# Routed experts on one core: tokens gathered for two units at once from a rounded and a rest part, biases by single-pass matmuls, eight places for weights

## The chip, the core and the metric

The kernel runs on one core of a Trainium2 chip. The metric is the device time of one execution in microseconds (us). The engines are TensorE (PE in the rows, its weight loads PEld), VectorE (DVE), ScalarE (ACT), GpSimd (POOL) and SyncE (SP), whose queue issues nearly all DMAs.

## The reference

One inference step of one layer on 384 tokens of width 1024 (128 context tokens, 256 latent tokens). The part that matters here is the expert sub-layer:

```python
logits = xt @ router_w + router_b
top_val, top_idx = lax.top_k(logits, 4)          # of 32 experts
gates = softmax(top_val)
# for each expert e, the tokens that chose it:
h = xblk @ w_gu[e] + b_gu[e]                      # 1024 -> 2048
x_glu, x_lin = split(h, 2)                        # both clipped at 7
act = x_glu * sigmoid(1.702 * x_glu) * (x_lin + 1)
y = act @ w_down[e] + b_down[e]                   # 1024 -> 1024
# y times the gate, summed per token; then x = LN(ALPHA * x + gate2 * y)
```

Ahead of it stand the conditioning, the mLSTM and Fourier heads and a first LayerNorm. Everything is f32; the weights of the 32 experts are 32 x 12.6 MB, read once.

## The kernel before

**Two phases.** The first some 240 us hold everything up to the router. The rest runs the experts in order of their load (`ORDER`), each with a fixed number of places for tokens: 128, 96, 64 or 32. Experts are packed into 17 units of 128 rows. Unit 0 holds two experts of 64; the others follow the string DACBACBACBACACCE: A is one expert of 128, B 96 + 32, C 64 + 64, D 64 + 32 + 32, E four of 32.

**A unit.** `marks` (DVE) writes a one-hot matrix `O`, token by place. `gather` multiplies it with the normalised tokens `tX`: for each of 8 groups of 128 channels, 3 token blocks, in plain f32; `modulate` (ACT for the first half, DVE for the second) applies scale and shift into `XT`. Unit 0 is gathered at the end of phase 1 (L985, XT0). A closure that `gather` returns, here called the spreader, transposes `O` and picks the gate values.

**An expert.** `gate_up` runs 8 channel steps (L1119), then adds the bias by matmuls (L1126) that pick the expert's row of `bgu` with a column of `PmQ`, broadcast. An expert has one or two "parts": parts of 64 rows use half of PE's columns and 512-column matmuls (n=2), parts of 32 rows a quarter and 256-column ones (n=4). Then `act`, the transposes (L1151), `down` (L1177) and the evictions (L1183 on ACT, L1185 on DVE). When a unit is complete `spread` (L1194, single pass) adds it into `yacc`.

**Weights.** They stream through nine places of 2 MB: pools ringh (two halves), ringq (2), ringr (1) and ringp (5), in a rotating list `rings`; four pieces per expert of w_gate_up, two of w_down. `load_gu` and `load_dn` issue them on SP in program order (L755), and each waits there for the last matmul that reads the place. The first expert's w_down has its second half in two other tiles (L781, L782).

**Order.** The program's order sets each engine's order. Matmuls are f32 (several passes inside) unless both operands are fp32r tiles, which take one pass; a value split into a rounded part and the rest then takes two matmuls.

Of the kernel before, what the change touches and what calls it, by code (L numbers as in the profile page):

```python
# [20 lines left out]
D = 1024  # L21
# [75 lines left out]
def tile_layer(ctx, tc, x_prompt, x_sample, state_C, state_n, state_m, c, c_ctx, w_ada, b_ada, w_in,  # L97
# [47 lines left out]
    tX = keep.tile([128, NB, D], FT, name="tX")  # L145
# [22 lines left out]
    SP.dma_start(tX[:, 1:3], x_sample.rearrange("o (b p) d -> p (o b) d", p=128))  # L168
# [21 lines left out]
    for i, w in enumerate(ada0):  # L190
        for a in range(2):
            SP.dma_start(w[:, :, 256 * a:256 * a + 256],
                         w_ada[0, :, 1024 * a + 256 * i:1024 * a + 256 * i + 256].rearrange("(k p) n -> p k n", p=128))
        if i == 0:
            SP.dma_start(tX[:, 0], x_prompt[0])
# [61 lines left out]
    with tc.tile_pool(name="psA", bufs=1, space=PSUM, reuse_waits="tile") as psA:  # L257
# [7 lines left out]
        def pos_x(b, hf):  # L265
# [3 lines left out]
            a = tX[:, b, hf * 512:hf * 512 + 512]  # L269
# [15 lines left out]
        def x_T(b):  # L285
            for q in range(2):
                p = bankA().rearrange("p (j n) -> p j n", j=4)
                for j in range(4):
                    PE.transpose(p[:, j], tX[:, b, (4 * q + j) * 128:(4 * q + j + 1) * 128], ident)
# [436 lines left out]
    PmQ = late.tile([128, 4, NE], FT, name="PmQ")  # L726
# [62 lines left out]
    def modulate(XT, i, pl, pc):  # L789

        for jj in range(4):
            j = 4 * i + jj
            if i:
                DVE.tensor_scalar(XT[:, j], pl[:, jj], aff[:, 1, j:j + 1], aff[:, 0, j:j + 1], op0=OP.mult, op1=OP.add)
            else:
                ACT.activation(XT[:, j], pl[:, jj], AF.Identity, bias=aff[:, 0, j:j + 1], scale=aff[:, 1, j:j + 1])
        DVE.tensor_add(XT[:, 4 * i:4 * i + 4], XT[:, 4 * i:4 * i + 4], pc)
# [27 lines left out]
    Pm = PmQ[:, 0]  # L825
    POOL.memset(PmQ, 0.0)
# [3 lines left out]
    with tc.tile_pool(name="psC", bufs=2, space=PSUM, reuse_waits="tile") as psC:  # L830
# [27 lines left out]
        def out_half(b, i):  # L858
            p, x = Pj.pop((b, i)), tX[:, b, halves[i]]
# [13 lines left out]
        def out_norm(b):  # L873
# [35 lines left out]
        def turn(b, i):  # L909
            pu = pu0.pop() if pu0 else psC.tile([128, 4, 128], FT, name="pu")  # L910
            for j in range(4):
                PE.transpose(pu[:, j], tX[:, b, (4 * i + j) * 128:(4 * i + j + 1) * 128], ident)
# [41 lines left out]
        def sort_1():  # L954
# [4 lines left out]
            DVE.tensor_scalar(Pm[:32], cst[:32, C_ROP:C_ROP + NE], cl[:, 2:3], None, op0=OP.is_equal)  # L959
# [6 lines left out]
        def sort_1b():  # L966
# [5 lines left out]
            for q in range(1, 4):  # L972
                DVE.tensor_copy(PmQ[32 * q:32 * q + 32, q], Pm[:32])
# [6 lines left out]
        def gather_0(b, *js):  # L980
            for jj in range(*js):
# [3 lines left out]
                PE.matmul(t[:, jj % 4], tX[:, b, jj * 128:(jj + 1) * 128], O0[:, b], start=(b < 2 and jj % 4 == 0), stop=(b != 1),  # L985
# [58 lines left out]
        XT0 = mo.tile([128, 8, 128], FT, name="XT")  # L1044
        for i in range(2):
            modulate(XT0, i, xt[i], xc[i])
# [10 lines left out]
    def marks(sizes, ccol):  # L1057
        O = mo.tile([128, NB, 128], FT, name="O", bufs=1)[:, :, :sum(sizes)]
        i = at = 0
        while i < len(sizes):  # L1060
            n = sizes[i]
            e = next((q for q in range(len(sizes) - i) if sizes[i + q] != n), len(sizes) - i)
            DVE.tensor_tensor(O[:, :, at:at + e * n].rearrange("p b (e s) -> p b e s", e=e), iota(n, e),
                              ccol[:, :, i:i + e].unsqueeze(3).to_broadcast([128, NB, e, n]), op=OP.is_equal)
            i, at = i + e, at + e * n
        return O

    def gather(u, sizes, ccol, gcol_, XT=None, O=None):

        e, m = len(sizes), sum(sizes)  # L1070
        O = marks(sizes, ccol) if O is None else O
        if XT is None:
            XT = mo.tile([128, 8, 128], FT, name="XT")
            for i in range(2):
                pl, pc = (bank().rearrange("p (c n) -> p c n", c=4)[:, :, :m] for _ in range(2))
                for jj in range(4):
# [3 lines left out]
        OT = mo.tile([128, T], FR, name="OT", bufs=3)[:m]  # L1080
        gc = mo.tile([128, 4], FT, name="gc", bufs=3)
        parts, at, c_ = [], 0, 0
        for n in sizes:

            parts.append([(at + o, t, c_ + q, o) for q, (o, t) in enumerate(PARTS[n])])
            at, c_ = at + n, c_ + len(PARTS[n])
        U[u] = dict(XT=XT, OT=OT, gc=gc, m=m, parts=parts)

        def spreader():
            p = bank()  # L1090
# [5 lines left out]
            for i in range(e):  # L1096
                for o, n, c_, _ in parts[i]:
# [6 lines left out]
    def gate_up(j, u, at, wts, bias, between={}):  # L1104
# [4 lines left out]
        banks = [[bank(), bank()] if t[1] == 2 else [bank()] for t in parts]  # L1109
        for n_, k in enumerate(ks):  # L1110
# [9 lines left out]
        for (o, n, _, _), p in zip(parts, banks):  # L1120
            m, f = 128 // n, 1024 // n
            for g_ in range(2):
                for h in range(n):
                    q, c_ = divmod(1024 * g_ + f * h, 512)
                    out = p[g_] if n == 2 else p[0][:, f * g_:f * g_ + f]
                    PE.matmul(out[m * h:m * h + m], bias[:, q:q + 1].to_broadcast([128, m]), bgu[:, c_:c_ + f], start=False, stop=True,  # L1126
                              skip_group_check=True)
# [60 lines left out]
    def spread(u):  # L1188
        y, OT = U[u]["y"], U[u]["OT"]
        for b in range(NB):  # L1190
            for hf in range(2):
                p = bank()
                for q in range(2):
                    PE.matmul(p, OT[:, b * 128:(b + 1) * 128], y[q][:, hf * 512:(hf + 1) * 512].bitcast(FR), start=(q == 0), stop=(q == 1))  # L1194
# [10 lines left out]
    def gather_unit(u, O=None):  # L1205
        cp, gp = code, gate
        return gather(u, SIZES[u], unit_cols(u, cp), unit_cols(u, gp), None if u else XT0, O)

# [42 lines left out]
    def second_bias(bdn):  # L1251
        for b in range(NB):
            for i in range(2):
                py, a = bank(), yacc[:, b, i * 512:(i + 1) * 512]
                PE.matmul(py, cT[:, 1, b], bdn[:, i * 512:(i + 1) * 512], start=True, stop=True)
                DVE.tensor_add(a, a, py)

    spread_0 = gather_unit(0)
# [11 lines left out]
    def fold(b):  # L1270

        for eng, hs in ((DVE, slice(0, 640)), (POOL, slice(640, 1024))):
            x, y = xw[:, hs], yacc[:, b, hs]
            eng.tensor_mul(x, tX[:, b, hs], fb[:, 2, hs])  # L1274
# [253 lines left out]
```

## Time and profile before

| | |
|---|---|
| three runs | 1280.65, 1282.75 (median), 1286.96 us |
| profiled execution | 1282.31 us, span in the profile 1280.5 us |
| PE busy | 1218.2 us, 95% of the span |
| DVE, ACT, POOL busy | 444.6, 232.7, 64.4 us |
| DMA | 452.78 MB, mean 354 GB/s |
| chain that ended last | PE 87%, DMA 5%, DVE 4% |

Busy time of PE includes matmuls whose ends are modelled, so starts are used for paces. The idle time before a group says what it waited for; on the queue of SP such a wait is a place that was not yet free.

### The profile page before, as it was taken

The page shows a single profiled execution, that of the slowest core. Times are in us where ns is not written, and L with a number is a line of the kernel's source. Part 1 is how long each engine was busy: PE and PEld are TensorE (multiplying, and loading weights), DVE is VectorE, ACT ScalarE, POOL GpSimd, SP SyncE. Part 2 cuts the span into 40 slices and gives each one's busy share as a digit, 9 for nine tenths or more (in the row PEclk, how much of TensorE's full clock was granted, in tenths as well). Part 3 has the DMA queues.
Part 4 walks back from the last instruction along what each step waited for, and adds up shares of the span by engine and source line. Part 5 has one row for each costly group of instructions (what it writes and reads, how often), then busy time and mean ns, then how long its engine had stood idle before and what let it go on. Part 6 is the DMA issues. An engine that isn't in the chain of part 4 may idle for free.

```text
span 1280.5 us, 17506 instructions
## 1 busy us (share of the span) xinstructions
PE 1218.2 (95%) x7180; PEld 586.9 (46%) x7180; DVE 444.6 (35%) x941; ACT 232.7 (18%) x446; POOL 64.4 (5%) x75
## 2 busy tenths in 40 slices
PE   7999989899999999999999999999999999997884
PEld 4967767543444343443424353434434343443321
DVE  4544775422213233222313142232323042232315
ACT  2433341211111111110102011111111011111112
POOL 2001062100000000000000000000000000000301
PEclk9999988999999999999999999999999999998988
DMA  9978558799999999999999899898899789999993
GB/s 323 392 290 292 199 190 304 268 389 394 417 417 417 417 417 408 376 344 338 396 333 417 327 356 362 358 384 353 334 355 415 270 348 356 416 418 416 417 409 112
DMA packets 96918, 452.78 MB, mean 354 GB/s; under 512 B 8244, under 2 KB 18696, under 8 KB 62020
## 3 DMA queue, kind: packets, MB, share of 16 engines
q1 hardware_dynamic: 94976, 449.91, 89.7%
q10 hardware_dynamic: 1268, 1.31, 0.3%
q8 instruction: 58, 0.95, 0.3%
q0 software_dynamic: 592, 0.42, 0.1%
q14 instruction: 24, 0.20, 0.0%
HBM read 448.91 MB, written 2.70 MB: 353 GB/s over the span
## 4 chain that ended last, share of the span: by engine, by line
PE 87%; DMA 5%; DVE 4%; ACT 1%; SPq 1%; issue 1%; ACTq 0%; DVEq 0%
PE b L1119 37%; PE b L1177 18%; PE b L1078 7%; PE b L1126 5%; PE b L1194 4%; PE p L421 3%; DMA w<-in_w_gate_up_dram 2%; PE pm L853 2%; PE b L1151 2%; DMA w<-in_ln_w_dram 2%; DMA w<-in_w_ada_dram 1%; PE k L352 1%; PE a L219 1%; PE b L1094 1%; PE n L553 1%
## 5 line engine op out<-in xcount | busy, mean ns | idle before, releaser
L1119 PE MATMUL b<-w,XT 128*64 128x512 f32 (+1 forms) x2560 | 492.8, 602 | 17.3 <-ACT w L1268 6.8
L1119 PEld LDWEIGHTS b<-w,XT 128*64 128x64 f32 (+1 forms) x2560 | 143.9, 129 | 318.9 <-issue 299.8
L1177 PE MATMUL b<-w,aT 128*64 128x512 f32 (+1 forms) x1596 | 245.4, 511 | 3.9 <-DMA w<-in_w_down_dram 3.7
L1137 DVE TENSOR_SCALAR g<-b 128x512 f32<-128x512 f32 (+1 forms) x40 | 24.4, 611 | 431.9 <-PE b L1126 428.9
L1177 PEld LDWEIGHTS b<-w,aT 128*64 128x64 f32 (+1 forms) x1596 | 81.1, 126 | 159.6 <-issue 140.8
L1185 DVE SCALAR_TENSOR_TENSOR y<-b,gc,y 64x512 fp32r<-64x512 f32 (+1 forms) x88 | 57.4, 652 | 220.8 <-ACT y L1183 220.6
L1183 ACT ACTIVATE y<-b,gc 64x512 fp32r<-64x512 f32 (+2 forms) x100 | 58.7, 587 | 313.9 <-PE b L1177 276.5
L1138 ACT ACTIVATE b<-g 128x512 f32<-128x512 f32 (+1 forms) x40 | 21.5, 538 | 385.2 <-DVE g L1137 384.6
L1078 PEld LDWEIGHTS b<-O,tX 128*128 128x128 f32 x768 | 87.0, 192 | 9.8 <-issue 9.8
L1078 PE MATMUL b<-O,tX 128*128 128x128 f32 x768 | 90.0, 277 | 0.0
L1126 PE MATMUL b<-bgu,PmQ 128*64 128x512 f32 (+1 forms) x416 | 64.5, 495 | 0.0
L1199 DVE TENSOR_TENSOR yacc<-yacc,b 128x512 f32<-128x512 f32 x90 | 55.0, 679 | 0.0
L1274 POOL TENSOR_TENSOR XT<-tX,w 128x384 f32<-128x384 f32 x3 | 3.0, 1005 | 909.5 <-DMA w<-in_w_gate_up_dram 909.5
L1194 PE MATMUL b<-y,OT 128*128 128x512 f32 x192 | 48.7, 402 | 0.0
L1194 PEld LDWEIGHTS b<-y,OT 128*128 128x128 f32 x192 | 34.8, 188 | 17.9 <-issue 6.9
L1152 ACT ACTIVATE aT<-b 128x512 f32<-128x512 f32 (+1 forms) x40 | 21.3, 534 | 116.5 <-PE b L1151 111.3
L1126 PEld LDWEIGHTS b<-bgu,PmQ 128*64 128x64 f32 (+1 forms) x416 | 21.8, 124 | 42.6 <-issue 40.6
L120 DVE TENSOR_TENSOR lw<-w,hw 128x1024 fp32r<-128x1024 f32 x20 | 24.4, 1222 | 35.9 <-ACT hw L119 35.6
L853 PE MATMUL pm<-w,mH 128*128 128x512 f32 x96 | 33.3, 429 | 0.0
L421 PE MATMUL p<-hw,uH 128*128 128x512 f32 x72 | 29.7, 412 | 1.7 <-ACT kq L411 1.7
L1151 PEld LDWEIGHTS b<-cst,g 128*128 128x128 f32 x136 | 14.3, 142 | 34.8 <-issue 28.3
L119 ACT ACTIVATE hw<-w 128x1024 fp32r<-128x1024 f32 x20 | 21.1, 1055 | 46.3 <-PE p L421 34.6
(368 smaller groups left out, 1028.3 us busy)
## 6 DMA issues: line engine op xcount, KB each, us to landing
w<-in_w_gate_up_dram SPq DMA_DIRECT2D x107, 2048.0 KB, 12.1
w<-in_w_down_dram SPq DMA_DIRECT2D x61, 2048.0 KB, 10.0
w<-in_w_gate_up_dram SPq DMA_DIRECT2D x42, 1024.0 KB, 12.0
w<-in_w_ada_dram SPq DMA_DIRECT2D x8, 2048.0 KB, 12.4
w<-in_w_ada_dram SPq DMA_DIRECT2D x8, 1024.0 KB, 13.2
w<-in_w_in_dram SPq DMA_DIRECT2D x4, 2048.0 KB
w<-in_w_out_dram SPq DMA_DIRECT2D x2, 2048.0 KB
w<-in_w_down_dram SPq DMA_DIRECT2D x4, 1024.0 KB, 27.9
```

The costliest lines, as they stand in the source:

```text
L120: (eng or DVE).tensor_sub(l, w, h.bitcast(FT))
L421: PE.matmul(p[b], x, y, start=(k == 0 and t == 0), stop=(k == 7 and t == 2))
L853: PE.matmul(pm, x, y, start=(n == 0 and t == (part == 0) and part != 1), stop=(n == 7 and t == 2 and part != 0))
L1078: PE.matmul((pl if b else pc)[:, jj], tX[:, b, (4 * i + jj) * 128:(4 * i + jj + 1) * 128], O[:, b], start=(b < 2), stop=(b != 1))
L1119: PE.matmul(p[g_][m * h:m * h + m], XT[:, k, o:o + m], rhs, start=(n_ == 0), stop=False, skip_group_check=True)
L1126: PE.matmul(out[m * h:m * h + m], bias[:, q:q + 1].to_broadcast([128, m]), bgu[:, c_:c_ + f], start=False, stop=True, skip_group_check=True)
L1151: PE.transpose(p[:, cc], s["act"][i][:, cc * 128:(cc + 1) * 128], ident)
L1177: PE.matmul(q[m * h:m * h + m, :f], aT[:, k, o:o + m], w[:, h * f:(h + 1) * f], start=(k == 0), stop=(k == 7))
L1183: ACT.activation(hi if plain else hi.bitcast(FR), dst, AF.Copy, scale=g)
L1185: DVE.scalar_tensor_tensor(y[1][o:o + m, h * f:(h + 1) * f].bitcast(FR), dst, g, hi, op0=OP.mult, op1=OP.subtract)
L1194: PE.matmul(p, OT[:, b * 128:(b + 1) * 128], y[q][:, hf * 512:(hf + 1) * 512].bitcast(FR), start=(q == 0), stop=(q == 1))
L1199: DVE.tensor_add(a, a, p)
```

## The change

Five things are altered.

1. `tX` becomes three tiles, one per token block. Between the first two steps of the first `gate_up`, `halve` makes of each block a rounded fp32r part `tH` and the rest `tL`.
2. `gather_two` gathers two units together, 8 times in place of 16: `O` is 256 wide, and for each group of channels and each token block there are two single-pass matmuls (tH, tL) of 256 columns: 48 per pair. The second unit's spreader runs in the middle of its first expert's `gate_up`.
3. The rows of `bgu` are read into the tile `aT` and split into two fp32r parts by ACT and DVE. For each expert DVE writes `pick`, the broadcast column, in fp32r. The bias takes single-pass matmuls: per n=2 part 8 of 256 columns, per n=4 part 2 of 512.
4. The experts' second bias (`bdn`) goes into the matmuls of `spread(0)`; it is read by SP into a weights' place.
5. The pool ringr is gone: eight places.

```diff
-    tX = keep.tile([128, NB, D], FT, name="tX")
+    tX = [keep.tile([128, D], FT, name=f"tX{b}") for b in range(NB)]
...
-    ringr = ctx.enter_context(tc.tile_pool(name="ringr", bufs=1, reuse_waits="tile"))
-    rings = [ringh, ringq, ringr, ringp, ringp, ringp, ringq, ringp]
+    rings = [ringh, ringq, ringp, ringp, ringp, ringq, ringp]
...
-        for name in ("aT", "y0"):
-            mo.tile([128, 1024], FT, name=name, bufs=1)
-        bgu = mo.tile([128, 512], FT, name="bgu", bufs=1)
+        bgu = mo.tile([128, 2, 512], FR, name="bgu", bufs=1)
+        raw = mo.tile([128, 512], FT, name="aT", bufs=1)
         for q in range(4):
-            POOL.dma_start(bgu[32 * q:32 * q + 32], b_gu[0, :, q * 512:(q + 1) * 512])
+            POOL.dma_start(raw[32 * q:32 * q + 32].rearrange("e (g n) -> e g n", g=2),
+                           b_gu[0].rearrange("e (g n) -> e g n", g=2)[:, :, 256 * q:256 * q + 256])
+        split(raw, bgu[:, 0], bgu[:, 1])
...
+    def halve(b):
+        low = mo.tile([128, D], FR, name="y0", bufs=1)
+        ACT.activation(tH[b], tX[b], AF.Copy)
+        DVE.tensor_sub(low, tX[b], tH[b].bitcast(FT))
+        tL.append(keep.tile([128, D], FR, name="tL", tag=f"tX{b}"))
+        POOL.tensor_copy(tL[b], low.bitcast(FT))
...
-            for i in range(2):
-                pl, pc = (bank().rearrange("p (c n) -> p c n", c=4)[:, :, :m] for _ in range(2))
-                for jj in range(4):
-                    for b in range(NB):
-                        PE.matmul((pl if b else pc)[:, jj], tX[:, b, (4 * i + jj) * 128:(4 * i + jj + 1) * 128], O[:, b], start=(b < 2), stop=(b != 1))
-                modulate(XT[:, :, :m], i, pl, pc)
+    def gather_two(O):
+        XT = mo.tile([128, 2, 8, 128], FT, name="XT", bufs=1)
+        for i in range(4):
+            pl, pc = (bank().rearrange("p (c n) -> p c n", c=2) for _ in range(2))
+            for jj in range(2):
+                for b in range(NB):
+                    for q, t in enumerate((tH, tL)):
+                        PE.matmul((pl if b else pc)[:, jj], t[b][:, (2 * i + jj) * 128:(2 * i + jj + 1) * 128], O[:, b],
+                                  start=(b < 2 and q == 0), stop=(b != 1 and q == 1))
+            halves_ = lambda t: t.rearrange("p c (q n) -> p c q n", q=2)
+            modulate(XT[:, :, 2 * i:2 * i + 2].rearrange("p q c n -> p c q n"), 2 * i, halves_(pl), halves_(pc), i % 2)
+        return XT[:, 0], XT[:, 1]
...
+        for n in {t[1] for t in parts}:
+            pick[n] = mo.tile([128, 4 // n, 128], FR, name=f"pick{n}", bufs=1)
...
-                    PE.matmul(out[m * h:m * h + m], bias[:, q:q + 1].to_broadcast([128, m]), bgu[:, c_:c_ + f], start=False, stop=True,
-                              skip_group_check=True)
+            for q in range(2):
+                if n == 4:
+                    PE.matmul(p[0], pick[4][:, 0], bgu[:, q], start=False, stop=(q == 1), skip_group_check=True)
+                else:
+                    for h in range(2):
+                        for g_ in range(2):
+                            PE.matmul(p[g_][:, 256 * h:256 * h + 256], pick[2][:, h], bgu[:, q, 256 * g_:256 * g_ + 256], start=False,
+                                      stop=(q == 1), skip_group_check=True)
...
+                if u == 0:
+                    PE.matmul(p, cT[:, 1, b], bdn[:, hf * 512:(hf + 1) * 512], start=True, stop=False)
...
-        inside = {2: [sort_2], 5: [sort_3]} if i == 0 else last_steps(ORDER[i - 1], SIZE[j] == 32)
+        inside = {0: [lambda: [halve(b) for b in range(NB)]], 2: [sort_2], 5: [sort_3]} if i == 0 else last_steps(ORDER[i - 1], SIZE[j] == 32)
+        if i and u in later:
+            inside.setdefault(4, []).append(later.pop(u))
...
-        if i == 3:
-            second_bias(bdn)
         if new:
-            gather_unit(v, O)()
+            later.update(zip(new, units(new, O)))
+            later.pop(v)()
         if i == 1:
-            bdn = mo.tile([128, 8, 128], FT, name="XT").rearrange("p k n -> p (k n)")[:32]
-            POOL.dma_start(bdn, b_dn[0])
+            bdn = slot(4, 1024, whole=True)[0][:32, 0]
+            SP.dma_start(bdn, b_dn[0])
```

On PE, at the end of the first expert and the first gather, stood before (`w`, `w_1945` and `y_1946` hold w_down; `b` is a PSUM bank):

```order
L1119 MATMUL b<-w,XT 64x512 x16
L1126 MATMUL b<-bgu,PmQ 64x512 x4
L1177 MATMUL b<-w,aT 64x512 x8
L1177 MATMUL b<-w_1945,aT 64x512 x6
L1177 MATMUL b<-y_1946,aT 64x512 x2
L1078 MATMUL b<-O,tX 128x128 x24
L1092 MATMUL b<-cst,O 128x128 x3
```

and now, at the same place:

```order
L1163 MATMUL b<-w,XT 64x512 x16
L1171 MATMUL b<-bgu,pick_2104 128x256 x8
L1222 MATMUL b<-w,aT 64x512 x8
L1222 MATMUL b<-w_1949,aT 64x512 x6
L1222 MATMUL b<-y_1950,aT 64x512 x2
L1107 MATMUL b<-O,tH_1940 128x256
L1107 MATMUL b<-O,tL 128x256
L1107 MATMUL b<-O,tH_1941 128x256
L1107 MATMUL b<-O,tL 128x256
L1107 MATMUL b<-O,tH_1942 128x256
L1107 MATMUL b<-O,tL 128x256
```

The 24 f32 matmuls of one unit (48 passes in the trace) become 48 single-pass ones of twice the columns for two units, each with a stationary tile of its own.

On ACT, where phase 2 begins, stood before:

```order
L880 ACTIVATE tX<-tX,m_1474 128x1024
L931 ACTIVATE gate<-tiny 128x32 x2
L796 ACTIVATE XT<-xt,aff 128x128 x4
L1236 ACTIVATE cT<-b 32x384 x2
L1138 ACT_TABLE_LOAD
L1138 ACTIVATE b<-g 128x512
```

and now:

```order
L880 ACTIVATE tX_71<-tX_71,m_1477 128x1024
L931 ACTIVATE gate<-tiny 128x32 x2
L119 ACTIVATE bgu<-aT 128x512
L796 ACTIVATE XT<-xt,aff 128x128 x4
L1065 ACTIVATE tH_1940<-tX_69 128x1024
L1065 ACTIVATE tH_1941<-tX_70 128x1024
L1065 ACTIVATE tH_1942<-tX_71 128x1024
L1285 ACTIVATE cT<-b 32x384 x2
```

The split of the bias rows (L119) now stands ahead of XT0's modulation, and three copies of 1024 columns behind it.

On SP, the end of the first expert's w_gate_up and its w_down stood before as

```order
L755 DMA w<-in_w_gate_up_dram 128x2x2048 x3
L755 DMA w<-in_w_down_dram 128x4x1024
L781 DMA w_1945<-in_w_down_dram 128x3x1024
L782 DMA y_1946<-in_w_down_dram 128x1024
L759 TENSOR_LOAD eidi
```

and now as

```order
L755 DMA w<-in_w_gate_up_dram 128x2x2048 x3
L755 DMA w<-in_w_down_dram 128x2x1024 x2
L781 DMA w_1949<-in_w_down_dram 128x3x1024
L782 DMA y_1950<-in_w_down_dram 128x1024
L759 TENSOR_LOAD eidi
```

The first half of w_down comes in two pieces because its place is now ringh, which the first two steps of the first `gate_up` read; before it was a ringp place that a matmul of phase 1 reads last. L781 and L782 stand behind it on SP.

## Rows read from the trace of the kernel before

**Rows 1.** The page: data rate in 40 slices, chain, two groups (busy, mean ns).

```profile
GB/s 323 392 290 292 199 190 304 268 389 394 417 417 417 417 417 408 376 344 338 396 333 417 327 356 362 358 384 353 334 355 415 270 348 356 416 418 416 417 409 112
...
PE b L1119 37%; PE b L1177 18%; PE b L1078 7%; PE b L1126 5%; PE b L1194 4%; PE p L421 3%; DMA w<-in_w_gate_up_dram 2%; PE pm L853 2%; PE b L1151 2%; DMA w<-in_ln_w_dram 2%; DMA w<-in_w_ada_dram 1%; PE k L352 1%; PE a L219 1%; PE b L1094 1%; PE n L553 1%
...
L120 DVE TENSOR_TENSOR lw<-w,hw 128x1024 fp32r<-128x1024 f32 x20 | 24.4, 1222 | 35.9 <-ACT hw L119 35.6
...
L119 ACT ACTIVATE hw<-w 128x1024 fp32r<-128x1024 f32 x20 | 21.1, 1055 | 46.3 <-PE p L421 34.6
```

**Rows 2.** Stretches of phase 2: span, PE, PEld, DVE, ACT, POOL busy, PEclk, DMA share, GB/s.

```profile
242.00:320.00 78.00, 77.30 (x430) 31.64 (x430) 20.66 (x59) 10.95 (x19) 3.36 (x5) 1.00 0.96 377
320.00:500.00 180.00, 180.00 (x1087) 75.09 (x1083) 50.14 (x103) 25.76 (x51) 0.00 (x0) 0.99 1.02 415
500.00:1100.00 600.00, 595.80 (x3497) 250.93 (x3491) 181.08 (x353) 83.83 (x164) 0.00 (x0) 1.00 0.92 359
1100.00:1248.00 148.00, 131.80 (x845) 51.49 (x849) 40.74 (x84) 22.43 (x44) 11.87 (x12) 0.92 1.02 415
1248.00:1280.50 32.50, 15.16 (x124) 6.42 (x116) 18.05 (x29) 7.91 (x16) 5.88 (x4) 0.82 0.31 116
```

**Rows 3.** Timeline of PE: one gather and the expert behind it.

```profile
1149.26 5.62 PE L1078 MATMUL b<-O,tX 128*128 128x128 f32 x48
1154.73 0.49 PE L1092 MATMUL b<-cst,O 128*128 128x128 f32 x3
...
1155.71 2.78 PE L1119 MATMUL b<-w,XT 128*32 128x512 f32 x24
```

**Rows 4.** Timeline of PE: single-pass matmuls of 384 columns, the first and last of 57.

```profile
59.20 0.33 PE L406 MATMUL p<-uH,hw 128*128 128x384 f32 x1
...
68.91 0.34 PE L406 MATMUL n<-uH,lw 128*128 128x384 f32 x1
```

**Rows 5.** Timeline of PE: biases of an n=2 and of an n=4 part, a spread.

```profile
257.29 1.89 PE L1126 MATMUL b<-bgu,PmQ 128*64 128x512 f32 x8
259.01 1.89 PE L1119 MATMUL b<-w,XT 128*64 128x512 f32 x8
...
1192.70 1.05 PE L1126 MATMUL b<-bgu,PmQ 128*32 128x256 f32 x16
1193.67 3.05 PE L1194 MATMUL b<-y,OT 128*128 128x512 f32 x12
```

**Rows 6.** Groups of PE by form: biases.

```profile
L1126 PE MATMUL b<-bgu,PmQ 128*64 128x512 f32 x224 | 52.1, 594 | 0.0
...
L1126 PE MATMUL b<-bgu,PmQ 128*32 128x256 f32 x192 | 12.6, 380 | 0.0
```

**Rows 7.** Timeline where phase 2 begins, all engines.

```profile
217.84 2.06 POOL L1037 DMA_DIRECT2D bgu<-in_b_gate_up_dram  x4 [0.29 <-POOL tX L887]
...
227.28 0.51 SPq L781 DMA_DIRECT2D w<-in_w_down_dram  x1
...
234.33 0.19 DVE L942 SCALAR_TENSOR_TENSOR gate<-gate,sel 128x32 f32<-128x32 f32 x1
...
238.23 1.51 ACT L796 ACTIVATE XT<-xt,aff 128x128 f32<-128x128 f32 x4 [5.99 <-PE xt L985]
...
240.62 3.65 PE L1119 MATMUL b<-w,XT 128*64 128x512 f32 x16 [1.42 <-issue]
```

**Rows 8.** Tile bgu: time from issue to landing.

```profile
DMA to landing us min/median/max: 5.0/5.5/5.9
```

**Rows 9.** Timeline, SP and PE: the final rows' constants, and PE behind them.

```profile
1163.57 5.49 SPq L1308 DMA_DIRECT2D w<-in_ln_w_dram  x1
...
1183.64 4.45 PE L1119 MATMUL b<-w,XT 128*32 128x512 f32 x24 [6.79 <-ACT w L1268]
```

**Rows 10.** Line L248, GpSimd over 1024 columns: ns min/median/max, first and last start.

```profile
L248 POOL TENSOR_TENSOR w<-w x8: 2397/2432/2465, 160.3 to 188.0; 128x1024 fp32r<-128x1024 f32 x8
```

**Rows 11.** Timeline of PE: first steps behind the gather that follows a unit B.

```profile
531.74 3.65 PE L1119 MATMUL b<-w,XT 128*64 128x512 f32 x16 [1.40 <-DVE XT L797]
```

More of the change, by code (lines that the diff above doesn't have):

```diff
@@ L1055, in bank @@
         return ps.tile([128, 512], FT, name="b")
[L1057 to L1065, printed above, removed]
-        return O
@@ new lines, in tile_layer, with marks @@
+    tL = []
+    def halve(b):
[4 more added lines that the diff above has]
+        POOL.tensor_copy(tL[b], low.bitcast(FT))
+    def marks(*units):
+        O = mo.tile([128, NB, 256], FR, name="O", bufs=1)
+        for q, (sizes, ccol) in enumerate(units):
+            i, at = 0, 128 * q
+            while i < len(sizes):
+                n = sizes[i]
+                e = next((q for q in range(len(sizes) - i) if sizes[i + q] != n), len(sizes) - i)
+                DVE.tensor_tensor(O[:, :, at:at + e * n].rearrange("p b (e s) -> p b e s", e=e), iota(n, e),
+                                  ccol[:, :, i:i + e].unsqueeze(3).to_broadcast([128, NB, e, n]), op=OP.is_equal)
+                i, at = i + e, at + e * n
+        return O
@@ new lines, in gather_one @@
+    def gather_one(O, m):
+        XT = mo.tile([128, 2, 8, 128], FT, name="XT", bufs=1)[:, 0]
+        for i in range(2):
+            pl, pc = (bank().rearrange("p (c n) -> p c n", c=4)[:, :, :m] for _ in range(2))
+            for jj in range(4):
+                for b in range(NB):
+                    out, cols, o = (pl if b else pc)[:, jj], slice((4 * i + jj) * 128, (4 * i + jj + 1) * 128), O[:, b, :m]
+                    if b == 0:
+                        PE.matmul(out, tX[0][:, cols], o.bitcast(FT), start=True, stop=True)
+                        continue
+                    for q, t in enumerate((tH, tL)):
+                        PE.matmul(out, t[b][:, cols], o, start=(b == 1 and q == 0), stop=(b == 2 and q == 1))
+            modulate(XT[:, 4 * i:4 * i + 4, :m], 4 * i, pl, pc, i)
+        return XT
@@ L1119, in gate_up @@
                         PE.matmul(p[g_][m * h:m * h + m], XT[:, k, o:o + m], rhs, start=(n_ == 0), stop=False, skip_group_check=True)
[L1120 to L1125, printed above, removed]
-                    PE.matmul(out[m * h:m * h + m], bias[:, q:q + 1].to_broadcast([128, m]), bgu[:, c_:c_ + f], start=False, stop=True,
-                              skip_group_check=True)
+        for (_, n, _, _), p in zip(parts, banks):
+            for q in range(2):
[6 more added lines that the diff above has]
+                                      stop=(q == 1), skip_group_check=True)
         S[j] = dict(banks=banks, act={})
@@ L1203, in unit_cols, with units @@
         return t[:, :, UNITS[u][0]:UNITS[u][-1] + 1]
-    def gather_unit(u, O=None):
-        cp, gp = code, gate
-        return gather(u, SIZES[u], unit_cols(u, cp), unit_cols(u, gp), None if u else XT0, O)
+    def units(us, O=None):
+        O = marks(*((SIZES[u], unit_cols(u, code)) for u in us)) if O is None else O
+        XTs = gather_two(O) if len(us) == 2 else (XT0,)
+        return [unit(u, SIZES[u], unit_cols(u, gate), XTs[q], O, q) for q, u in enumerate(us)]
     done = {u: 0 for u in range(len(UNITS))}
@@ L1249, in sort_3 @@
         DVE.tensor_copy(iti, pe_[:1, 0:ITEMS + 1])
[L1251 to L1258, printed above, removed]
+    later = dict(zip((0,), units((0,))))
     load_dn(ORDER[0])
@@ L1311, in tile_layer @@
             load_dn(ORDER[i + 1])
-        gate_up(j, u, UNITS[u].index(j), [WT.pop(("g", j, q)) for q in range(4)], PmQ[:, :, j], inside)
+        gate_up(j, u, UNITS[u].index(j), [WT.pop(("g", j, q)) for q in range(4)], PmQ[:, j], inside)
         if i == 0:
@@ L1316, in tile_layer @@
         if new:
-            started.add(v)
+            started.update(new)
             if i <= 1:
-                O = marks(SIZES[v], unit_cols(v, code))
+                O = marks(*((SIZES[q], unit_cols(q, code)) for q in new))
         while ready:
@@ L1483, in tile_layer @@
         wts = Stream(ds(SP.value_load(iti[0:1, ds(i, 1)], min_val=0, max_val=NE - 1), 1))
-        gather("x", [32], cc[:, 0:3].unsqueeze(2), cc[:, 3:6].unsqueeze(2))()
-        gate_up("x", "x", 0, wts, oc[:, 0:4])
+        O = marks(([32], cc[:, 0:3].unsqueeze(2)))
+        unit("x", [32], cc[:, 3:6].unsqueeze(2), gather_one(O, 32), O)()
+        gate_up("x", "x", 0, wts, ob)
         act_T("x", "x", 0, 0)
```

114 lines of the change are left out of this document (63 added, 51 removed).

## The prediction

> **What bounds the kernel now.** I read the page's chain first: it is 87% PE by the table above, and the gathers (L1078) and biases (L1126) hold 7% and 5% of it [rows 1]. That reads like a kernel bound by PE alone, in which any PE time removed comes off the end. The row of data rates spoils this: many slices stand at 415 to 418 GB/s and none higher [rows 1]. The stretches make it exact [rows 2]. From 320 to 500 us, and again from 1100 to 1248 us, DMA moves 415 GB/s for 180 and 148 us on end: there the weights are at their limit, and the places are refilled as soon as PE frees them. Only from 500 to 1100 us is the rate 359: the queue of SP waits for places.
>
> So two resources share the bound, and the account must be kept in both. At 416 GB/s the 215.4 MB of the middle stretch (600 x 359) need 518 us, so DMA stands idle there for 82 us; in 242 to 320 another 7 us. All the data of phase 2 are 384.7 MB by the five stretches, less 1.5 MB of output: 383.2 MB or 921 us. Check: 242 + 921 + 89 of idle = 1252, and after 1248 only 3.8 MB move [rows 2], 1.5 of them output, so the weights end at about 1253. From there to the span's end 27.3 us remain (the last expert's matmuls and the final rows), and 1.8 us lie outside the span (1282.31 against 1280.5; the median of the three runs, 1282.75, is 0.4 us above, so I make no correction).
>
> **What PE saves.** A gather before is 48 passes from 1149.26 to the next row at 1154.73: 5.47 us, 0.114 us a pass with its own weight load [rows 3]. 16 of them are 87.5 us. After, 8 times 48 single-pass matmuls of 256 columns. No row shows one of 256 columns. Bounds: 56 steps of 384 columns from 59.20 to 68.91 give 0.173 us, each with a new stationary tile of 128 columns [rows 4]; a pass of 128 columns takes 0.114 [rows 3], which may be a floor. In proportion to columns 256 take 0.116 and 512 take 0.231; twelve of 512 in a spread take 3.05 us with the modelled end of the last, at most 0.25 each [rows 5], so the proportion holds upward. The range is 0.114 to 0.173, and I take 0.116, because 256 lies between a row that obeys the proportion and one that equals its result. 384 matmuls: 44.5 us. Saved 43 us.
>
> A bias of an n=2 part is 1.72 us start to start (8 matmuls), one of an n=4 part 0.97 us (16) [rows 5]. There are 224/8 = 28 and 192/16 = 12 parts [rows 6]. After: 8 x 0.116 = 0.93 and 2 x 0.231 = 0.46 us. Saved 28 x 0.79 + 12 x 0.51 = 28 us. The second bias in spread(0) costs PE the same six matmuls as before. Sum on PE: 71 us, 69 of them before the last stretch.
>
> **What is added.** (a) Start of phase 2. The rows of bgu were issued on POOL at 217.84 [rows 7]. Their tile is now `aT`, whose memory the router's last small tiles held, so the four issues wait for DVE L942 at 234.4. Four issues of 0.5 us and a landing of 5.5 us as before [rows 8] end at about 242. ACT's split stands in its queue ahead of XT0's modulation, which began at 238.23 [rows 7], and DVE's half ahead of DVE's. So the first gate_up begins at about 244.6, not 240.62. PE has then been idle for over 5 us; behind the 6.79 us wait that ended at 1183.64, 24 matmuls took 4.45 us and not 2.78 [rows 3, 9], so I add such a slow start here: +6 us; bounds +2 and +8. (b) `halve`: three ACT copies of 1024 columns, three subtractions on DVE, three casts on POOL, linked through one tile y0, and ahead of sort_2 on DVE, for which PE waits inside the same gate_up. By 1.06 and 1.22 us [rows 1] and 2.43 us on POOL [rows 10] the third subtraction ends 1.06 + 3 x 1.22 + 2 x 2.43 = 9.6 us after the start, while PE's first two steps take 3.65 us [rows 7]: a stall of up to 6 us, none if POOL's cast is much shorter than that product or sort_2 needs little of DVE. Taken 3. (c) gather_two needs all eight PSUM banks and waits for the last evictions of the expert before. The wait behind the three units B was 1.40 us per gather [rows 11]. Two pairs now follow a B and two an A; with the eviction of one more bank I take 1.9 and 1.3 us for them, 6.4 in place of 4.2: +2; bounds 0 and 10. (d) The marks of 256 places, the picks and the extra adds of the final rows run on DVE, busy in the middle stretch for 181 us of 600 [rows 2], under PE's matmuls, so I cost them at nothing; without that cover the 40 picks alone would cost up to 24 us at 0.61 each, half of DVE's 1.22 for 1024 columns [rows 1].
>
> (e) The weights. w_down of the first expert was issued from 226.9, its second half at 227.28 [rows 7]. Its place is now ringh, free only when two steps of the first gate_up are done, at about 248, and its second half (L781, L782) and every later load stand behind it on SP. 4.2 MB that moved between 227 and 238 now move after 249. DMA then starts 7 us later with 4.2 MB (10 us) more. (f) A place less: PE may be one load less behind DMA, and DMA one less ahead: 2.1 MB, 5 us at the end.
>
> **The sum.** By PE alone: 1282.3 - 71 + 6 + 3 + 2 = 1222. By data alone: 249 + 387.4/0.416 = 1180 for the last weight, + 27.3 + 1.8 = 1209 with no idle. Neither can be reached, since idle time of DMA before is tied to PE's pace in the middle. In 500 to 1100 there lie 11 of the 16 gathers (528 of 768 passes) and 16 us of the bias gain: 47 us. Idle of DMA there: 82 - 47 = 35. At 500 us DMA is 9 us behind its old self (249 + 260 for 108.3 MB against 500), and PE about 3 us ahead (20 us saved by then, less 11 for (a) to (c), the rest spent waiting for weights, since that stretch was at the limit): 12 less, 23. New waits (c) +2, one place less (f) +5: 30. Near the end the constants of the final rows, issued at 1163.57 for which PE waited 6.79 us [rows 9], now meet a PE that comes earlier while the places are full: I put +8 for it (bounds 0, and 20, three times the old wait). Idle 38. The weights end at 249 + 931 + 38 = 1218, the span at 1245, the run at **1247**. The same along PE: the last unit begins at 1155.71 [rows 3] less 43 (gathers) and 24 (biases up to there), plus 11 for (a) to (c) and some 9 of waiting for weights: 1109. Before, the weights ended 97 us after that point; with 5 and 8 as above, 1219, one us from the other way. Its own range, with (a) +2 to +8, (c) 0 to 10 and the constants 0 to 20, is 1232 to 1262.
>
> So of 71 us on PE half is predicted to arrive; the rest turns into waits for weights and constants.
>
> A rule that speaks against the change: a load of weights overlaps matmuls in flight only when the row group differs (the Trainium skill, TensorE: Matmul & The Clock Gate, The mechanism), and the page puts the load of P columns at P/1.2 ns, 107 ns for 128. By it a 256-column matmul with a load of its own would take about 0.21 us, as an estimate from that page, and the run would come out at about 1295; the rows with 48 loads in 5.47 us [rows 3] show loads under the passes, so I hold it unlikely here.
>
> **The rivals.**
> R1, all of PE's saving arrives: data is no limit where I count it, because PE's lead in the middle fills the places early. Against: 415 GB/s over 180 us [rows 2]. It needs the idle of (f) and the constants to vanish and the offset at 500 to be 0: 1212 to 1222.
>
> R2, DMA can't carry more over long stretches than it did in the middle. Then all of phase 2 keeps 359 GB/s there, PE waits more, and the time stays at 1276 to 1289. For it: 359 over 600 us [rows 2]. Against: 415 over 148 and 180 us [rows 2]. By the Trainium skill (DMA: Bandwidth & Descriptors, Specifications) a core gets about 358 GB/s of HBM; the trace shows 415 for long stretches, so it does not bind here.
>
> R3, opposite sign: the 256-column matmul does not hide its load or runs at a lower rate, beyond 0.19 us. Place: L1107 and L1171. At 0.228, twice a pass of 128 columns [rows 3], the 384 of the gathers cost 87.5 us as before and the 224 of the n=2 parts 51, 3 more than before; PE gains 3 with the n=4 parts and pays 11 for (a) to (c), and the place less and the constants add up to 13: 1290 to 1303. The 608 matmuls eat the 71 us down to these 24 at 0.116 + 47/608 = 0.19 us; from there it decides. For it: no row at 256 columns. Against: the proportion up to 512 columns [rows 4, 5].
>
> R4, eight places and the new waits eat the gain again: w_down late for the first experts, gathers that wait for banks, the constants at 20 us, each at the far bound: 1262 to 1285. For it: where the rate is below its limit it is places that lack [rows 2], so every place counts.
>
> **How the numbers follow.** Forecast 0.60; R1 0.13; R2 0.04; R3 0.09; R4 0.14. About 0.5% (6.4 us) is what a measurement of this kernel can tell from no change. Faster: all of the forecast and R1, four fifths of R4: 0.84. Same: R2 and the rest of R4, and a bit of R3: 0.08. Slower: 0.08. The range leaves out R3, R2 and R4's last fifth above (0.16) and the lowest part of R1 below (0.04): 1216 to 1275.
>
> **What the profile after would show.** L1107: 48 starts in 5.5 to 5.7 us, 8 times; 0.2 us a start would be R3. L1171: 0.93 us per n=2 part. The first gate_up at about 244 to 245. Data rates of 380 to 400 in what was the middle stretch, and no slice above 418. L1163 and L1222 waiting for DMA more than before; a longer wait behind L1268's successor. The prediction is wrong if the middle stretch keeps 359 GB/s with PE waiting on something else, or if PE, now short of weights, spends long stretches at the slow pace seen behind a wait [rows 9].

## The result, and the profile after

The changed kernel takes 1245.94 us (median of 4 runs, 1240.41 to 1248.78) against 1284.45 us for the kernel before (4 runs beside it): ratio 0.9697, 95% interval 0.9654 to 0.9741. It is 38.5 us faster; 1247 was forecast. The profiled execution took 1248.78 us, its span is 1247.1 us.

The page of the changed kernel, first the data rate in 40 slices, then the chain, as in [rows 1]:

```profile
GB/s 324 391 277 263 216 174 255 156 389 406 404 416 417 416 417 417 416 407 414 415 362 409 414 363 358 419 416 362 363 417 398 301 391 403 406 418 403 401 410 118
...
PE b L1163 38%; PE b L1222 19%; PE b L1241 4%; PE p L422 3%; DMA w<-in_w_gate_up_dram 3%; PE b L1107 3%; PE b L1171 2%; PE pm L853 2%; DMA w<-in_ln_w_dram 2%; PE b L1196 2%; DMA w<-in_w_ada_dram 1%; PE k L353 1%; ACT y L1228 1%; PE a L220 1%; DVE y L1230 1%
```

Gathers and biases fell from 7% and 5% of the chain to 3% and 2% (the n=4 biases, L1167, are too small for the list). No slice is above 419 GB/s. The stretches, as in [rows 2], the last two cut at 1212 us, where the rate falls in this run:

```profile
242.00:320.00 78.00, 74.90 (x394) 32.72 (x398) 29.72 (x73) 14.34 (x24) 6.42 (x8) 0.98 0.92 366
320.00:500.00 180.00, 179.15 (x997) 68.86 (x993) 45.27 (x94) 25.27 (x46) 0.00 (x0) 0.95 1.02 415
500.00:1100.00 600.00, 596.39 (x3372) 248.22 (x3365) 190.03 (x372) 83.80 (x150) 1.01 (x1) 1.00 0.98 392
1100.00:1212.00 112.00, 80.67 (x528) 28.34 (x526) 31.67 (x67) 16.67 (x33) 12.89 (x13) 0.86 1.00 407
1212.00:1247.00 35.00, 17.44 (x140) 7.68 (x140) 18.05 (x29) 7.92 (x16) 5.88 (x4) 0.79 0.40 148
```

This is the picture that the prediction drew: the middle stretch went from 359 to 392 GB/s, and the stretches at the limit stayed at 415 and 407. After 1212 us 5.2 MB move, 1.5 of them output, so the weights end some 9 us later, at 1221 (1218 was forecast), and 26 us of tail remain.

What each operation costs now, on PE (a gather's first matmul and the row behind its last; an n=2 bias and the row behind; an n=4 bias and the first spread):

```profile
288.77 0.39 PE L1107 MATMUL b<-O,tH 128*128 128x256 f32 x1
...
294.63 0.49 PE L1130 MATMUL b<-cst,O 128*128 128x128 f32 x3
...
262.64 1.21 PE L1171 MATMUL b<-bgu,pick 128*128 128x256 f32 x8
263.79 1.94 PE L1163 MATMUL b<-w,XT 128*64 128x512 f32 x8
...
326.12 0.73 PE L1167 MATMUL b<-bgu,pick 128*128 128x512 f32 x2
326.79 1.12 PE L1239 MATMUL b<-w,cT 32*128 32x512 f32 x2
...
342.51 9.62 PE L1222 MATMUL b<-w,aT 128*64 128x512 f32 x32
```

48 matmuls of two units take 5.86 us, 0.122 each. A bias of an n=2 part takes 1.15 us from start to start (some 1.05 where a spread follows), one of an n=4 part 0.67 (0.57). The first spread, with the second bias inside, runs from 326.79 to 342.51: 15.7 us.

What PE waits for now:

```profile
PE b L1163 <- ACT w L1310: 19.7, 1, 19.7
PE b L1163 <- DMA w<-in_w_gate_up_dram: 7.7, 5, 3.9
...
PE b L1107 <- DVE y L1230: 4.5, 4, 1.4
...
PE b L1222 <- DMA w<-in_w_down_dram: 3.2, 2, 2.6
```

The numbers are the sum in us, the count and the longest. The wait for the constants of the final rows has grown from 6.79 us [rows 9] to 19.7; the gathers wait four times for a bank (DVE's evictions y). The table puts the 19.7 us down to ACT, but ACT itself waits there for a transfer, the one from `in_ln_w` (L1353) with which SP claims a weights' place for the constants and which stands among the weights on SP's queue:

```profile
1148.70 0.60 ACT L1310 ACTIVATE w<-b 128x512 f32<-128x512 f32 x1 [22.40 <-DMA w<-in_ln_w_dram]
```

Where phase 2 begins, as in [rows 7]:

```profile
237.21 2.23 POOL L1037 DMA_DIRECT2D aT<-in_b_gate_up_dram  x4 [16.55 <-issue]
...
246.87 3.05 SPq L755 DMA_DIRECT2D w<-in_w_down_dram  x2
249.97 0.46 SPq L781 DMA_DIRECT2D w<-in_w_down_dram  x1
...
241.26 0.63 ACT L119 ACTIVATE bgu<-aT 128x512 fp32r<-128x512 f32 x1 [7.24 <-DVE eidi L964]
241.80 1.49 ACT L796 ACTIVATE XT<-xt,aff 128x128 f32<-128x128 f32 x4
...
244.17 5.35 PE L1163 MATMUL b<-w,XT 128*64 128x512 f32 x16 [3.14 <-issue]
249.45 0.22 PE L1273 MATMUL b<-cl,cst 32*32 32x1 f32 x2
...
254.12 0.14 DVE L1274 COPY cl<-b 32x1 f32<-32x1 f32 x1
...
257.12 0.27 PE L1296 MATMUL b<-itm,cst 32*1 32x64 f32 x2
```

The split and XT0's modulation stand behind the rows of b_gate_up, the first w_down is issued 20 us later than before, and the first 16 passes take 5.35 us and not 3.65. PE does not wait in front of sort_2 (L1273), nor in front of sort_3 (L1296), which reads what sort_2's DVE part (from L1274) has made.

### The profile page after: what moved, and what is told of

Same layout as the page of the kernel before. It is cut to its first block, busy times and chain, and to the rows that moved or that the text cites. A ratio compares the mean times of both kernels' runs of the same rounds, so it can differ in the third digit from the quotient of the medians.

```text
span 1247.1 us, 16409 instructions
## 1 busy us (share of the span) xinstructions
PE 1167.6 (94%) x6628; PEld 556.8 (45%) x6628; DVE 446.4 (36%) x944; ACT 229.0 (18%) x418; POOL 69.3 (6%) x79
## 4 chain that ended last, share of the span: by engine, by line
PE 84%; DMA 7%; DVE 5%; ACT 2%; issue 1%; SPq 1%; ACTq 0%; DVEq 0%
PE b L1163 38%; PE b L1222 19%; PE b L1241 4%; PE p L422 3%; DMA w<-in_w_gate_up_dram 3%; PE b L1107 3%; PE b L1171 2%; PE pm L853 2%; DMA w<-in_ln_w_dram 2%; PE b L1196 2%; DMA w<-in_w_ada_dram 1%; PE k L353 1%; ACT y L1228 1%; PE a L220 1%; DVE y L1230 1%
## 5 line engine op out<-in xcount | busy, mean ns | idle before, releaser
L1163 PE MATMUL b<-w,XT 128*64 128x512 f32 (+1 forms) x2560 | 496.2, 604 | 30.5 <-ACT w L1310 19.7
L1222 PE MATMUL b<-w,aT 128*64 128x512 f32 (+1 forms) x1596 | 248.3, 515 | 3.3 <-DMA w<-in_w_down_dram 3.2
L1107 PE MATMUL b<-O,tH 128*128 128x256 f32 x192 | 47.7, 289 | 4.5 <-DVE y L1230 4.5
L1107 PE MATMUL b<-O,tL 128*128 128x256 f32 x192 | 46.5, 283 | 0.0
L1107 PEld LDWEIGHTS b<-O,tH 128*128 128x128 f32 x192 | 36.7, 191 | 10.2 <-DVE y L1230 5.3
L1107 PEld LDWEIGHTS b<-O,tL 128*128 128x128 f32 x192 | 36.7, 191 | 0.0
L1171 PEld LDWEIGHTS b<-bgu,pick 128*128 128x128 f32 x224 | 28.0, 189 | 18.7 <-issue 18.7
L1171 PE MATMUL b<-bgu,pick 128*128 128x256 f32 x224 | 32.8, 292 | 0.0
## 6 DMA issues: line engine op xcount, KB each, us to landing
w<-in_w_gate_up_dram SPq DMA_DIRECT2D x30, 1024.0 KB, 13.5
```

Of the source, the lines that this page charges most:

```text
L1107: PE.matmul((pl if b else pc)[:, jj], t[b][:, (2 * i + jj) * 128:(2 * i + jj + 1) * 128], O[:, b], start=(b < 2 and q == 0), stop=(b != 1 ...
L1163: PE.matmul(p[g_][m * h:m * h + m], XT[:, k, o:o + m], rhs, start=(n_ == 0), stop=False, skip_group_check=True)
L1171: PE.matmul(p[g_][:, 256 * h:256 * h + 256], pick[2][:, h], bgu[:, q, 256 * g_:256 * g_ + 256], start=False, stop=(q == 1), skip_group_che ...
L1222: PE.matmul(q[m * h:m * h + m, :f], aT[:, k, o:o + m], w[:, h * f:(h + 1) * f], start=(k == 0), stop=(k == 7))
```

## The experiments

Two theories. **Two accounts**, that of the prediction: both PE's work and the weights' transfer set the end, so PE time removed counts only where places are waited for. **PE alone**: the end moves by what PE's own work and its waits for other engines change; the shortfall from 71 us to 38.5 would then be costs on PE that the forecast missed. The result alone does not tell them apart: with what the rows show, 40 and 22 us saved, 9 lost in the first spread, 5 at the start and 13 more behind the constants, PE alone gives 1284 - 62 + 27 = 1249. Nor can any run do so afterwards, once its waits are counted, because the span is always the sum of PE's busy and idle time, and the wait for the constants, listed under ACT, is one for a transfer. The theories differ in what they forecast for an edit. All ratios are to the kernel before, about 1284.5 us; differences between two experiments are differences of their ratios times that. The intervals reach 0.002 to 0.003 to each side, some 3 us, and 0.004 for the changed kernel. So a difference between two experiments is known to some 4 us, one from the changed kernel only to some 6.

**1. A place less, alone.**

```diff
-    ringr = ctx.enter_context(tc.tile_pool(name="ringr", bufs=1, reuse_waits="tile"))
...
-    rings = [ringh, ringq, ringr, ringp, ringp, ringp, ringq, ringp]
+    rings = [ringh, ringq, ringp, ringp, ringp, ringq, ringp]
```

> The kernel before with the pool ringr taken out: eight places for weights, nothing else changed. Two accounts (PE's work and the weights' transfer both set the end): 5 us more (2.1 MB at 0.417 GB/ms less in hand when the last units begin), up to 12 if the place is also missing in the stretch from 320 to 500 us. PE alone (the end moves by what PE's own work and waits for other engines change): no difference, within 2 us.

1294.02 us, ratio 1.0063 (1.0044 to 1.0082): 8.1 us slower. PE has the same work, and PE alone forecast no difference; the price of a place is 8 us, where the prediction took 5. The wait for the constants grew here from 6.8 to 13.5 us, so the loss shows on PE too, as a wait for a transfer.

**2. The new biases alone, with eight places.** The kernel of experiment 1 with `split`, `pick` and the matmuls of the change; the split stands behind the modulation.

> The kernel before with eight places and the new bias matmuls, its split put behind XT0's modulation; gathers, second bias and all else as before. By the starts in the changed kernel a part of 64 rows takes 1.1 us and not 1.72, one of 32 rows 0.62 and not 0.97: 22 us of PE in all. Two accounts: 14 to 17 us faster than the kernel before with eight places, so 2 to 12 us faster than the kernel before. PE alone: 22 us faster than the kernel before.

1275.85 us, ratio 0.9925 (0.9906 to 0.9945): 9.6 us faster than before, 17.7 faster than experiment 1. Of 22 us on PE some 80% arrive. The rate from 500 to 1100 rose from 358 in experiment 1 to 369:

```profile
500.00:1100.00 600.00, 595.79 (x3461) 261.82 (x3455) 183.36 (x375) 83.63 (x163) 0.00 (x0) 0.99 0.93 369
```

**3. The gathers alone.** The changed kernel with the old biases (`bias.bitcast(FT)[:, q:q + 1].to_broadcast([128, m])` against an f32 `bgu`), whose rows are read as in the kernel before.

> The changed kernel with the old f32 bias matmuls and the rows of b_gate_up read where they were read before; gathers of two units, second bias in the first spread and eight places stay. Both theories: 16 to 20 us slower than the changed kernel, so 16 to 22 us faster than the kernel before; first matmul of phase 2 about 3 us earlier than in the changed kernel.

1265.52 us, ratio 0.9842 (0.9823 to 0.9862): 18.6 us slower than the changed kernel. The first gate_up begins at 239.92, 4.25 us earlier. Against experiment 1 the gathers, with the second bias in the first spread, bring 28.4 us, some 70% of the 40 that they save on PE; with the 17.7 of the biases 46, and the changed kernel stands 47.0 below experiment 1. The two parts add up.

**4. Biases left out.** The loop of bias matmuls in `gate_up` is gone, so b_gate_up is not added; `stop` moves to the last channel step.

```diff
-                        PE.matmul(p[g_][m * h:m * h + m], XT[:, k, o:o + m], rhs, start=(n_ == 0), stop=False, skip_group_check=True)
-        for (_, n, _, _), p in zip(parts, banks):
-            for q in range(2):
...
+                        PE.matmul(p[g_][m * h:m * h + m], XT[:, k, o:o + m], rhs, start=(n_ == 0), stop=(n_ == 7), skip_group_check=True)
```

> The changed kernel with the bias matmuls of gate_up left out (b_gate_up is not added): 38 us of PE less (28 parts of 1.1 us, 12 of 0.62). Two accounts: 18 to 23 us faster than the changed kernel, with waits of PE for weights longer by the rest and the rate in the middle stretch up from 392 to 405 or more. PE alone: 35 to 38 us faster than the changed kernel.

1217.23 us, ratio 0.9465 (0.944 to 0.9489): 29.8 us faster than the changed kernel, between the two expectations; its interval of 6 us reaches that of PE alone and just misses the other, so this run does not decide. The middle:

```profile
500.00:1100.00 600.00, 594.82 (x3290) 233.57 (x3286) 197.02 (x391) 85.65 (x152) 1.02 (x1) 1.00 1.01 410
```

392 to 410 GB/s over 600 us is 26 us of DMA's idle time, at 416 GB/s, and accounts for most of the 29.8. PE's waits for weights hardly grew (8.3 and 4.1 us in its table of waits, 7.7 and 3.2 in the changed kernel). So of 38 us of PE time removed across the units 78% arrive, as the biases' did in experiment 2. The prediction's share of two thirds (47 of 71 us, what lies between 500 and 1100 us) looks too low, and the 18 to 23 us expected here with it, though the interval reaches two thirds too.

**5. Split behind the modulation.** The rows are read into tile g, free early, and the call of `split` moves behind the loop that modulates XT0.

```diff
+        for name in ("aT", "y0"):
+            mo.tile([128, 1024], FT, name=name, bufs=1)
+        raw = mo.tile([128, 512], FT, name="g", bufs=1)
...
-        raw = mo.tile([128, 512], FT, name="aT", bufs=1)
...
-        split(raw, bgu[:, 0], bgu[:, 1])
...
+        split(raw, bgu[:, 0], bgu[:, 1])
```

> The changed kernel with the rows of b_gate_up read into tile g, whose memory is free early, and the split put behind XT0's modulation on ACT and DVE. First gate_up 3 us earlier and its first 16 passes in 3.65 us, not 5.35. Both theories: 3 to 6 us faster than the changed kernel; if the start delay costs nothing in the end, within 1 us.

1244.28 us, ratio 0.97 (0.9677 to 0.9723). Its first matmuls:

```profile
240.46 3.65 PE L1165 MATMUL b<-w,XT 128*64 128x512 f32 x16 [1.38 <-issue]
```

The mechanism is as forecast (3.7 us earlier and at full pace), but no gain can be told from the ratios; the medians differ by 1.7 us. Both theories expected 3 to 6, or 1 at most if the late start costs nothing. Inconclusive: a gain of 3 is inside the interval, and the term (a) of +6 is at its edge and not seen.

**6. Constants one expert later.**

```diff
-        if i == NE - 4:
+        if i == NE - 3:
             for at, r in enumerate((0, 1, 4, 5)):
                 final_row(at, r, fb)
```

> The changed kernel with the matmuls and copies of the final rows' constants one expert later, so that PE doesn't wait 19.7 us for them. Two accounts: the weights of the last four experts move at 407 GB/s of at most 418 there, so waits for weights of 10 to 17 us take the place: 2 to 8 us faster than the changed kernel. PE alone: 13 to 20 us faster.

1247.92 us, ratio 0.9705 (0.968 to 0.9731): no difference, where two accounts expected 2 to 8 us. PE's waits in it:

```profile
PE b L1163 <- DMA w<-in_w_gate_up_dram: 15.1, 7, 3.9
PE b L1222 <- DMA w<-in_w_down_dram: 7.9, 4, 3.7
```

The 19.7 us are gone, and waits for weights grew from 10.9 to 23.0. In the last stretch it is the weights that set the time: from 1100 to 1212 us the rate is 415 where it was 407. A wait of 20 us on the busiest engine cost nothing that can be told: with it gone PE waits 12 us more for weights, and it is busy for 7 us longer with the same matmuls (1174.8 us, where it was 1167.6). PE alone, which asked for 13 us or more, falls here; of all the runs this one and experiment 8 weigh most against it.

**7. Second bias apart.** As before: six matmuls and six additions of its own at `i == 3`.

```diff
-                if u == 0:
-                    PE.matmul(p, cT[:, 1, b], bdn[:, hf * 512:(hf + 1) * 512], start=True, stop=False)
...
+        if i == 3:
+            second_bias(bdn)
```

> The changed kernel with the second bias in six matmuls and six additions of its own behind the fourth gate_up, as before, and not between the matmuls of the first spread. In the changed kernel the first spread and the w_down behind it took 15.7 and 9.6 us of PE, before spread, second bias and w_down 3.0, 5.8 and 7.1: 9 us of PE less. Two accounts: the weights are at 410 to 418 GB/s in that stretch, so 0 to 5 us faster than the changed kernel. PE alone: 9 us faster.

1248.54 us, ratio 0.9707 (0.9681 to 0.9733): no difference, though PE's time is saved: the spread starts at 325.82 and the w_down behind it takes its usual 7.09 us. From the spread's start to the end of the first 24 passes of the next gate_up PE needs 21.2 us, where the changed kernel needs 28.0. Then it waits 4 us for weights, and 16 passes behind that take 5.27 us and not 3.65.

```profile
325.82 2.88 PE L1239 MATMUL b<-y,OT 128*128 128x512 f32 x12
328.64 7.09 PE L1222 MATMUL b<-w,aT 128*64 128x512 f32 x32
335.65 6.55 PE L1302 MATMUL b<-w,cT 32*128 32x512 f32 x12
...
355.41 1.93 PE L1222 MATMUL b<-w,aT 128*32 128x256 f32 x32 [0.98 <-DMA w<-in_w_down_dram]
360.39 5.27 PE L1163 MATMUL b<-w,XT 128*64 128x512 f32 x16 [3.05 <-DMA w<-in_w_gate_up_dram]
```

It lies where the weights are at 415 GB/s. Again no gain from PE's time can be told; PE alone expected 9 us.

**8. The three edits together.**

> The changed kernel with the three edits together (split behind the modulation, constants one expert later, second bias apart). Two accounts: 7 to 16 us faster than the changed kernel. PE alone: 25 to 33 us faster.

1242.8 us, ratio 0.9683 (0.9664 to 0.9701): 1.8 us below the changed kernel, inside both intervals, less than the 7 to 16 us of two accounts and far from the 25 to 33 of PE alone.

**9. Another string of units.** If the weights limit the first and the last units and PE those between, a unit that needs more PE than weights should stand right ahead of the last one, so that the places are full when it begins.

```diff
-SEQUENCE = "DACBACBACBACACCE"
+SEQUENCE = "DACBACBACBACCCAE"
```

> The changed kernel with the string of units DACBACBACBACCCAE in place of DACBACBACBACACCE: the last unit A, which needs more of PE than of weights, stands right ahead of E, which needs more weights than PE; the two units C come earlier. PE's work and the bytes are the same. Two accounts: places are filled during that A, so fewer waits for weights in E: 10 to 14 us faster than the changed kernel. PE alone: no difference, within 2 us.

1233.13 us, ratio 0.9602 (0.9578 to 0.9626): 12.2 us faster than the changed kernel with the same matmuls and the same bytes.

```profile
500.00:1100.00 600.00, 596.38 (x3381) 247.36 (x3380) 189.18 (x380) 82.70 (x148) 1.02 (x1) 1.00 1.00 403
```

The middle runs at 403 GB/s and not 392: 16 us less idle on DMA. Two accounts expected 10 to 14 us, PE alone nothing. The gain shows on PE as well: the wait for the constants went from 19.7 to 4.7 us, and those for weights hardly changed (9.0 where they were 10.9). Removing that wait by moving the constants gave nothing (6); here it is nearly gone, which fits transfers that run further ahead of PE.

**10. The same string in the kernel before.**

> The kernel before with the same string of units. Two accounts: it too waits for weights only behind 1155 us, so 7 to 10 us faster than the kernel before. PE alone: no difference, within 2 us.

1275.68 us, ratio 0.9936 (0.9913 to 0.9959): 8.2 us faster, inside the 7 to 10 of two accounts, and from 359 to 373 GB/s in the middle. So the gain of the string isn't owed to the change; whether 12 is more than 8 the intervals don't tell.

**11. New string, three edits, and the loads into w0 and y1 ahead of the first half of w_down.**

```diff
+        if j == ORDER[0]:
+            w, w1 = keep.tile([128, 3, D], FT, name="w0", tag="B"), mo.tile([128, D], FT, name="y1", bufs=1)
+            src = w_dn[0, ex, 512:1024].rearrange("o (k p) n -> p (o k) n", p=128)
+            SP.dma_start(w, src[:, 0:3])
+            SP.dma_start(w1, src[:, 3])
...
```

> The changed kernel with the new string, the three edits of the version tried last (split behind, constants later, second bias apart), and the second half of the first w_down (tiles w0 and y1) issued on SP ahead of its first half, so that 2.1 MB move between 227 and 247 us. Two accounts: 3 from the three edits as measured and 0 to 5 from the loads, 3 to 8 us faster than with the new string alone. PE alone: the loads change nothing; 3 us faster.

1228.08 us, ratio 0.9565 (0.9544 to 0.9586): 4.8 us faster than the string alone. How much is the loads' and how much the edits' was not separated.

**12. The string CCACCBADABBACCAE on top.**

> The same with the string CCACCBADABBACCAE: units that need more weights than PE stand first, while the weights are at their limit anyway, and units A and B are spread over the rest. Two accounts: 5 to 12 us faster than the run before this one. PE alone: no difference, within 2 us.

1221.21 us, ratio 0.9507 (0.9486 to 0.9528): 7.5 us faster than experiment 11, the fastest kernel with the whole computation here, 24 us below the changed one.

## Why the prediction was right, point by point

**What bounds the kernel.** Right, and shown: PE time removed near either end, work in 7 and a wait in 6, gave nothing that can be told; PE work removed along all units paid at 70 to 80% (2, 3, 4); and reordering without removing any work gave 12 us (9).

**The pace of 256 columns.** Forecast 0.116, measured 0.122 (the first of a group takes 0.22). With 384 matmuls and four waits for banks of 4.5 us the gathers cost 51 us in place of 92; saved 40, forecast 43 less 2 for (c). R3 needed 0.19 and is out. So is, here, the rule of the Trainium skill (TensorE: Matmul & The Clock Gate, The mechanism) that the prediction quotes against the change, by which a load overlaps matmuls only when the row group differs: 0.122 us hold a pass and a load of all rows together.

**The biases.** Mis-sized: 1.15 and 0.67 us a part and not 0.93 and 0.46: 28 x 0.57 to 0.68 and 12 x 0.30 to 0.40, some 22 us saved and not 28. Inside a group the pace is that of a gather: from the second matmul (262.87) on the starts are 0.12 us apart. The first step takes 0.23 and the one to the f32 matmul behind 0.21, and these two steps at the edges of a group make up the 0.22 us over the forecast. A gather has only the longer first step, and spreads it over 48 matmuls.

**(a) The start.** On PE as forecast: 244.17 (244.6), and 1.7 us more for the slow first passes. In the end no gain from undoing it can be told (5).

**(b) halve.** Forecast 3, measured 0 on PE, but not as reasoned. The prediction let PE wait for sort_2 itself; the matmul of sort_2 (249.45) reads what DVE had made before `halve` (in experiment 5 it starts 1 us ahead of the first subtraction). What stands behind the three subtractions on DVE is sort_2's own DVE part, from 254.12, and PE needs it only in sort_3, at 257.12. POOL's cast took 1.03 us and not the 2.43 of its product, so it was done by then.

**(c) Banks.** 4.5 us in four waits, forecast 6.4.

**The second bias "costs PE the same".** This step failed. Inside the spread it took 15.7 us with the spread, and 2.5 us of the w_down behind it, against 3.0 and 5.8 apart before: 9.4 us more, of which 1.2 go back, as the gate_up behind the second bias was that much slower before. The same six matmuls did not cost the same in another place. It cost nothing that can be told in the end only because it stands where the weights are at their limit (7).

**(e) The first w_down.** Issued at 246.87, its second half at 249.97, where 248 and 249 were forecast. Moving the second half ahead was tried only with other edits (11).

**(f) A place less.** 8.1 us (1), forecast 5.

**The constants.** Forecast 8 us of DMA's idle and up to 20; PE waited 19.7, DMA stood idle for 112 x (1 - 407/416) = 2.4 us, and moving them changed nothing (6).

**Idle of DMA in the middle.** Forecast 30 us, measured 600 x (1 - 392/416) = 35. With the 2.4 above 37 against 38: the two misses cancel, and so the sum hit 1247 more closely than its terms deserve. PE's saving, smaller than forecast, and the share of it that arrived, larger than forecast, cancel too. That the time was hit to 1 us is luck; that only about half of the 71 us arrived is what the mechanism asks for. The range of 1232 to 1262 does not follow from its bounds either, which add up to 14 below and 22 above, 1233 to 1269; the measured time lies in both.

R1 is out, as 70 to 80% of less than 71 us arrived and 8 us went for the place. R2 is out: 410 GB/s over 600 us in experiment 4. R4 did not come about; its parts were priced at 8 (place), 0 (constants) and 0 to 2 (start).

## What to carry to other kernels

With an engine some 95% busy and a transfer at its limit in some stretches, price an edit where it lies: the same microsecond of PE was worth 0.7 to 0.8 spread over all units and nothing that can be told in another place, and a wait of 20 us behind a limited transfer cost nothing that could be told. When a tuned order was balanced for the old costs, a cheaper step shifts the balance, and moving one unit (12 us here) can bring as much as the next edit of the engine. Read the data rate by stretch ahead of the chain, which shows PE in both cases.

## What the runs showed of the hardware that was not expected

PE's granted clock fell to 0.50, its lower level of 1.2 GHz, while PE was busy without a pause, in the first spread of the changed kernel, where f32 matmuls of 32 rows (L1239) alternate with full ones. Stretches of the changed kernel, PE alone (busy, clock, DMA share, GB/s):

```profile
326.00:331.00 5.00, 5.00 (x16) 0.96 1.01 419
331.00:345.00 14.00, 14.00 (x22) 0.50 1.01 418
```

Ahead of the fall PE ran those matmuls, and it rose again only in the w_down behind: 0.67 from 345 to 349 us, 1.00 from 349. With the twelve passes in a row and behind the w_down, as in experiment 7, the w_down kept its pace, and the clock fell within them and rose only in the gate_up behind:

```profile
328.60:335.60 7.00, 7.00 (x33) 1.00 1.01 421
338.00:340.00 2.00, 2.00 (x6) 0.95 1.00 418
340.00:346.00 6.00, 6.00 (x23) 0.50 1.01 411
```

In the kernel before, with the same order, it was 0.58 from 338 to 341 us. That the 32 rows are the cause was not isolated.

A cast of 1024 columns from f32 to fp32r on GpSimd took 1.03 us, less than half of a product of the same size [rows 10].
